# A hybrid decoder layer: experts in a written order per engine, the per-layer-input product moved ahead of the experts, w_out tile by tile

## The chip, the cores and the metric

The kernel runs on one core of a Trainium2 chip. The metric is the device time of one execution in microseconds (us), lower is better. The engines are named as in the profile: PE (TensorE, matrix products and transposes), DVE (VectorE), ACT (ScalarE), POOL (GpSimd, here mostly indirect DMAs) and SP (SyncE, which issues the other DMAs). Each engine works through its own instructions in their order and waits for others by semaphores.

## The reference

One layer over 1024 tokens of width 1024, in float32. After two parallel mixers, which the change leaves alone:

```
x = x + merged @ w_out
h = rmsnorm(x, ln_moe)
group = top-1 of 4 groups; experts = top-2 of its 8 (32 experts in all)
for each chosen expert e:  hid = silu(h @ w_gate[e]) * (h @ w_up[e]);  y = hid @ w_down[e]
x = x + sum over the two experts of weight * y
x = x + sigmoid(rmsnorm(x, ln_ple) @ w_ple_gate) * (p @ w_ple_proj)
out = rmsnorm(x, ln_final)
```

w_out and w_ple_gate are 1024x1024, w_ple_proj is 256x1024, each expert has 1024x512 (gate), 1024x512 (up) and 512x1024 (down).

## The kernel before

A float32 product is made of three passes: each operand is split into a high part (ACT copies it to the rounded type fp32r) and a low part (DVE subtracts the high part from the original), and PE adds high*high, high*low and low*high in PSUM. So each weight passes through ACT (`wh`) and DVE (`wl`) before PE reads it.

**w_out and routing** (`w_out`, L905). 16 products, each of one tile of 128 tokens and one half n of 512 columns (24 matmuls of 512 columns): first all eight tiles with n=0, then all eight with n=1, into PSUM tiles "mm" and "c" in turn, two buffers each. DVE adds the loaded `x` to a product (L931). `route_logits` (L987) transposes the new x on PE and multiplies by the router weights; with n=1 a tile's routing follows (`route_tile`), a long series of small DVE operations that ends in two matmuls `ps_py<-ro,so`. These are generators; one step of each open one runs after every third matmul, and `ROUTE_LAG` puts steps between the parts. After the last tile the indices of the first experts' tokens (`gidx`) exist, and POOL gathers the rows `xg` from DRAM (`h2d`).

**Experts** (`moe`, L1285). Each of 32 experts has at most 88 rows here. The parts run in the order u(e), g(e+1), d(e): up, the next expert's gate, down. Each part is 24 matmuls over four splits of 128x1024 (u0..u3 and so on, six matmuls each); `wh` and `wl` have three buffers each (L1181), so a split may start once the matmuls of the split three earlier are done. Between them PE transposes the next rows (`ps_c<-identk,xg`; ACT copies `xh`, DVE makes `xl`) and the hidden values (`ps_w<-identk,gu`; then `hh`, `hl`). `sg` is the silu of the gate on ACT, `gu` its product with up on DVE. The output `y` is scaled out of PSUM half by ACT (L1242) and half by DVE (L1243), and scattered to DRAM (`yb`). The weights arrive as blocks `mraw` of 2 MB in eight buffers. What stands where on an engine is decided by a scheduler that builds the program, from the order in the code and its own estimates.

**Per-layer-input product.** `ple_in` (L1350) splits p and w_ple_proj and makes 16 products of six matmuls (`ps_c<-wpp,pT`), which ACT scales into `ppo` in SBUF (L1391). It is advanced by `step` inside the expert loop, some of the weight blocks being given up for it (`KEEP`).

**Tail** (L1490 on). w_ple_gate is split to `pgh`, `pgl` (L1485, L1486), the scattered rows are read back (`yin`) and added to x (L1406), and eight tiles are multiplied, gated with `ppo` and normalised.

Of the kernel before, what the change touches and what calls it, by code (L numbers as in the profile page):

```python
# [71 lines left out]
class Kern:  # L72
# [646 lines left out]
    def common(self, ctx):  # L719
# [19 lines left out]
        self.yb = dp.tile([2 * S, D], F32, name="yb")  # L739
        self.ovt = dp.tile([NOV * CAP, 4], F32, name="ovt")  # L740
# [164 lines left out]
    def w_out(self, pool, w, rt):  # L905

        nc, a = self.nc, self.a
        tags = ("mm", "c")
# [9 lines left out]
        for s in range(2 * NT):  # L918
            n, i = s // NT, s % NT
            (wh, wl), tok, sl = w[n], slice(i * 128, i * 128 + 128), slice(n * 512, n * 512 + 512)  # L920
            x = xs[i][n] = pool.tile([128, 512], F32, name="x2", bufs=10)
# [16 lines left out]
            side.append(self.route_logits(pool, rt, i, x, r, n))  # L938
        while side:
            run()  # L940
# [46 lines left out]
    def route_logits(self, pool, rt, i, x, r, q):  # L987

        nc = self.nc
        yield 1  # L990
# [6 lines left out]
        yield 1  # L997
        pl = self.logits[:, 36 * i:36 * i + 36]
        for k in range(4):
            self.mm(pl, hT[:, k, :], self.wr[:, 4 * q + k, :], start=(q == 0 and i == 0 and k == 0),  # L1000
                    stop=(q == 1 and k == 3), skip=True)
        yield 1
        if q == 1:
            yield from self.route_tile(rt, i, r, pl)

    def route_tile(self, rt, i, r, pl):
# [35 lines left out]
        for _ in range(ROUTE_LAG):  # L1042
            yield 1
# [20 lines left out]
        yield 1  # L1064
        yield 1
# [219 lines left out]
    def moe(self, mo, keep):  # L1285
# [5 lines left out]
        raws = [(self.expert_raw(w, z), z) for w, z in zip(order, "1110000x")]  # L1291
        n, free = [8, 0], {"0": 0, "1": 0, "x": 0}

        def raw():

            r, z = raws.pop(0)
            n[1] += 1
            if n[1] > KEEP[z][free[z]]:
                free[z] += 1
            elif n[0] < len(order):  # L1300
                raws.append((self.expert_raw(order[n[0]], z), z))
                n[0] += 1
            return r
        ple = self.ple_in()
        last = [0]

        def step(e):
            if free["1"] > 0 and (last[0] < 1 or e >= last[0] + 3) and (free["1"] > 2 or last[0] == 0):
                if last[0] == 0:
                    last[0] = e  # L1310
                next(ple, None)
# [8 lines left out]
        nx = {}  # L1320

        def rows(e):
            nx["x"] = self.expert_rows(mo, xgs[e % 3])
            gath(e + 3)

        def hidden(e, sg):
            nx["h"] = self.expert_hidden(mo, sg)
        rows(0)
        x = nx["x"]
        sg = self.expert_gate(mo, x, raw())  # L1330
        for e in range(NE):
            more = e + 1 < NE
            sg = self.expert_up(mo, x, raw(), sg, (lambda: rows(e + 1)) if more else None)
            step(e)
            if more:
                x = nx["x"]
                nsg = self.expert_gate(mo, x, raw(), lambda: hidden(e, sg))
            else:
                hidden(e, sg)
            self.expert_down(mo, nx["h"], raw(), self.sidx[:, e:e + 1], self.sw[:, e:e + 1])  # L1340
            sg = nsg
            if e % 3 == 0:
                step(e)
        for _ in ple:
            pass


    def ple_in(self):
# [22 lines left out]
        self.ple = th, tl, hi, lo  # L1371
        self.pps = []
        for i in range(NT):
            if i % 4 == 0:
                ob = self.blk("10"[i // 4], "ppo")
            self.pps.append(ob[:, i % 4 * D:i % 4 * D + D])
            for n in range(2):
                self.ple_proj(i, n)
                yield

    def ple_proj(self, i, n):

        th, tl, wh, wl = self.ple
# [7 lines left out]
        self.nc.scalar.activation(self.pps[i][:, n * 512:n * 512 + 512], p, AF.Copy, scale=0.5)  # L1391
# [76 lines left out]
    def load_pg(self, mo):  # L1468
# [4 lines left out]
        st = self.blk("x", "pgr")  # L1473
        raws = [st[:, n * D:n * D + D] for n in range(4)] + self.xgs + [mo.tile([128, D], F32, name="pgr7", tag="y", bufs=3)]
        prev = self.rawdma
        for k0, k1 in ((0, 6), (6, 8)):
# [3 lines left out]
            for k in range(k0, k1):  # L1480
                if k % 4 == 0:
                    hi, lo = (self.blk("10"[k // 4], f"pg{c}{k}", F32R) for c in "hl")
# [8 lines left out]
    def tail(self, pool, mo, out):  # L1491
        nc, a = self.nc, self.a
        pg = self.load_pg(mo)
        next(pg)
        lnf = mo.tile([128, D], F32, name="lnf", tag="y", bufs=3)
        xs = {0: self.tail_x(pool, mo, 0)}
        pg.send(self.yin)
        nc.sync.dma_start(lnf, a["ln_final"][None, :].to_broadcast([128, D]))
        fr = {0: self.tail_front(pool, mo, *xs.pop(0))}
        xs[1] = self.tail_x(pool, mo, 1)  # L1500
        for i in range(NT):
            if i + 2 < NT:
# [14 lines left out]
    def post_mixer(self, out):  # L1517
        tc, nc = self.tc, self.nc
        with ExitStack() as ctx:
            keep = ctx.enter_context(tc.tile_pool(name="keep", bufs=1))  # L1520
            self.big["1"] = (ctx.enter_context(tc.tile_pool(name="big1", bufs=1)), 3)
            with tc.tile_pool(name="big2", bufs=1) as b2:
# [10 lines left out]
                with tc.tile_pool(name="op", bufs=1, side="right") as op:  # L1533
                    self.w_out(op, w, rt)
# [93 lines left out]
```

## Time and profile before

| | us |
|---|---|
| median of 3 runs | 1698.07 (1697.37 to 1699.02) |
| the profiled execution | 1698.45 |
| its span (first to last instruction) | 1696.6 |
| outside the span | 1.85 |
| PE busy | 1618.1 |
| DVE busy | 1279.7 |
| ACT busy | 863.0 |

Rows of the trace count from the start of the span. The last product of w_out is done at 956, the first matmul of an expert starts at 977, the last expert's down part at 1570, the tail's products at 1591. A matmul's own duration of about 0.39 overlaps its neighbours; what counts is the distance of starts.

### The profile page before, as it was taken

The page shows a single profiled execution, that of the slowest core. Times are in us where ns is not written, and L with a number is a line of the kernel's source. Part 1 is how long each engine was busy: PE and PEld are TensorE (multiplying, and loading weights), DVE is VectorE, ACT ScalarE, POOL GpSimd, SP SyncE. Part 2 cuts the span into 40 slices and gives each one's busy share as a digit, 9 for nine tenths or more (in the row PEclk, how much of TensorE's full clock was granted, in tenths as well). Part 3 has the DMA queues.
Part 4 walks back from the last instruction along what each step waited for, and adds up shares of the span by engine and source line. Part 5 has one row for each costly group of instructions (what it writes and reads, how often), then busy time and mean ns, then how long its engine had stood idle before and what let it go on. Part 6 is the DMA issues. An engine that isn't in the chain of part 4 may idle for free.

```text
span 1696.6 us, 26475 instructions
## 1 busy us (share of the span) xinstructions
PE 1618.1 (95%) x9856; PEld 1225.6 (72%) x9856; DVE 1279.7 (75%) x2636; ACT 863.0 (51%) x1389; POOL 156.5 (9%) x134
## 2 busy tenths in 40 slices
PE   7999999999999999999899699999999999999697
PEld 5877777777787878778687466666666666666586
DVE  7256665377788888666608889999998888899785
ACT  5234333332233333322313388888887777888442
POOL 1000000000000000000002312112211111111000
PEclk9999999999999999999999899999999999999799
DMA  6333222332323323368837689999799989999651
GB/s 191 103 108 100 70 74 82 109 100 79 78 55 94 79 76 88 110 212 267 262 113 265 226 311 335 384 372 380 286 360 349 346 300 349 344 386 362 218 175 50
DMA packets 189030, 349.75 MB, mean 206 GB/s; under 512 B 50862, under 2 KB 123182, under 8 KB 164322
## 3 DMA queue, kind: packets, MB, share of 16 engines
q1 hardware_dynamic: 179682, 331.02, 56.3%
q0 software_dynamic: 9216, 17.01, 3.2%
q8 instruction: 78, 1.28, 0.3%
q14 instruction: 54, 0.44, 0.1%
HBM read 301.10 MB, written 52.95 MB: 209 GB/s over the span
## 4 chain that ended last, share of the span: by engine, by line
PE 81%; DVE 9%; DMA 5%; issue 2%; ACT 2%; SPq 1%; POOL 0%; DVEq 0%; ACTq 0%; POOLq 0%
PE ps_mm L77 47%; PE ps_py L77 16%; PE ps_c L77 9%; PE ps_w L81 4%; PE ps_w L77 4%; PE ps_c L81 1%; DVE so L1068 1%; DMA raw<-in_w_out_dram 1%; DMA ysp<-yaT 1%; DMA mraw<-in_w_up_e_dram 1%; DMA x<-in_x_dram 0%; DMA zr<-zT 0%; DVE wl L1187 0%; ACT sm L337 0%; DMA yb<-y,idx 0%
## 5 line engine op out<-in xcount | busy, mean ns | idle before, releaser
L1187 DVE TENSOR_TENSOR wl<-mraw,wh 128x1024 fp32r<-128x1024 f32 x384 | 457.8, 1220 | 51.0 <-ACT wh L1186 49.9
L1186 ACT ACTIVATE wh<-mraw 128x1024 fp32r<-128x1024 f32 x384 | 402.7, 1058 | 96.0 <-PE ps_mm L77 66.2
L77 PE MATMUL ps_mm<-h,wh 128*128 128x512 f32 x1152 | 378.7, 403 | 0.1
L77 PEld LDWEIGHTS ps_mm<-h,wh 128*128 128x128 f32 x1152 | 214.3, 189 | 47.4 <-issue 1.6
L77 PE MATMUL ps_mm<-h,wl 128*128 128x512 f32 x576 | 231.1, 401 | 0.0
L77 PE MATMUL ps_mm<-wh,xh 128*88 128x512 f32 x512 | 205.3, 401 | 0.0
L77 PE MATMUL ps_mm<-wl,xh 128*88 128x512 f32 x512 | 204.1, 399 | 1.3 <-DVE wl L1187 1.2
L77 PE MATMUL ps_mm<-wh,xl 128*88 128x512 f32 x512 | 201.8, 394 | 0.0
L77 PEld LDWEIGHTS ps_mm<-h,wl 128*128 128x128 f32 x576 | 108.8, 189 | 23.4 <-issue 1.0
L1244 POOL DMA_INDIRECT yb<-y,idx x32 | 71.4, 2230 | 462.6 <-ACT wh L1186 255.0
L77 PEld LDWEIGHTS ps_mm<-wl,xh 128*88 128x88 f32 x512 | 79.4, 155 | 40.5 <-DVE wl L1187 5.0
L77 PEld LDWEIGHTS ps_mm<-wh,xl 128*88 128x88 f32 x512 | 79.4, 155 | 37.2 <-DVE xl L1163 0.2
L77 PEld LDWEIGHTS ps_mm<-wh,xh 128*88 128x88 f32 x512 | 79.3, 155 | 35.0 <-issue 0.4
L77 PE MATMUL ps_py<-wl,hh 128*88 128x512 f32 x256 | 102.7, 401 | 0.0
L77 PE MATMUL ps_py<-wh,hl 128*88 128x512 f32 x256 | 100.3, 393 | 0.5 <-DVE hl L1228 0.5
L77 PE MATMUL ps_py<-wh,hh 128*88 128x512 f32 x256 | 99.4, 393 | 0.6 <-ACT hh L1227 0.6
L102 ACT ACTIVATE wh<-raw 128x1024 fp32r<-128x1024 f32 x44 | 46.6, 1058 | 100.4 <-PE ps_mm L77 95.2
L103 DVE TENSOR_TENSOR wl<-raw,wh 128x1024 fp32r<-128x1024 f32 x42 | 51.3, 1220 | 60.9 <-ACT wh L102 60.5
L77 PEld LDWEIGHTS ps_py<-wl,hh 128*88 128x88 f32 x256 | 39.4, 154 | 27.2 <-DVE wl L1187 10.0
L77 PEld LDWEIGHTS ps_py<-wh,hh 128*88 128x88 f32 x256 | 39.5, 154 | 20.4 <-ACT hh L1227 0.7
L77 PEld LDWEIGHTS ps_py<-wh,hl 128*88 128x88 f32 x256 | 39.5, 155 | 17.9 <-DVE hl L1228 0.9
L77 PE MATMUL ps_mm<-woh,m 128*128 128x512 f32 x128 | 47.0, 417 | 1.3 <-ACT m L93 1.3
(398 smaller groups left out, 2877.5 us busy)
## 6 DMA issues: line engine op xcount, KB each, us to landing
mraw<-in_w_gate_e_dram SPq DMA_DIRECT2D x64, 1024.0 KB, 8.8
mraw<-in_w_up_e_dram SPq DMA_DIRECT2D x64, 1024.0 KB, 8.6
mraw<-in_w_down_e_dram SPq DMA_DIRECT2D x64, 1024.0 KB, 8.5
raw<-in_w_in_dram SPq DMA_DIRECT2D x36, 512.0 KB, 4.1
gT<-t SPq DMA_DIRECT2D x32, 256.0 KB, 2.0
g<-gT SPq DMA_DIRECT2D x32, 256.0 KB, 4.5
yin<-yb SPq DMA_DIRECT2D x16, 512.0 KB, 5.2
zT<-t SPq DMA_DIRECT2D x28, 256.0 KB, 2.0
```

Source lines behind the costliest of these rows:

```text
L77: return self.nc.tensor.matmul(out, l, r, start=start, stop=stop, skip_group_check=skip)
L81: return self.nc.tensor.transpose(out, in_, self.ident[:k, :k])
L102: nc.scalar.activation(wh, raw, AF.Copy)
L103: (eng or nc.vector).tensor_tensor(wl, raw, wh.bitcast(F32), op=ALU.subtract)
L1068: V.tensor_scalar(so, cb[:, CB["iota"]][:, :CAP], pk[:, k:k + 1], None, op0=ALU.is_equal)
L1186: nc.scalar.activation(wh, r, AF.Copy)
L1187: nc.vector.tensor_sub(wl, r, wh.bitcast(F32))
L1244: nc.gpsimd.indirect_dma_start(out=self.yb[:, :], out_offset=bass.IndirectOffsetOnAxis(ap=sidx, axis=0), in_=y, in_offset=None, bounds_che ...
```

## The change

`w_out` now takes both halves of a tile one after the other, all into the PSUM tile "mm", and the lags of the last tile's routing are shorter. Loading and splitting of the per-layer-input operands move into `w_out`; eight of the 16 products are issued beside the end of the routing, the other eight after it, ahead of the experts. Their results go to a DRAM tensor `ppd` by SP and are read back in the tail. In the expert stage every ACT, DVE and PE instruction is chained to the one before it, in the order in which `experts` is written. Both halves of `y` are on ACT and stand three splits after the products that they read. All eight blocks stay with the weights.

```diff
-KEEP = {"1": (29, 36, 36, 999), "0": (50, 999), "x": (0, 999)}
+NP_ROUTE = 8
...
+        self.ple = self.ple_in(pool)
...
-            n, i = s // NT, s % NT
+            n, i = s % 2, s // 2
...
+            if s in (4, 7, 9, 11):
+                next(self.ple)
...
-            p = self.ptile(tags[s % 2])
+            p = self.ptile("mm")
...
+        for _ in range(NP_ROUTE):
+            run()
+            next(self.ple)
...
-        for _ in range(ROUTE_LAG):
+        for _ in range(ROUTE_LAG if i < NT - 1 else 4):
             yield 1
...
-        raws = [(self.expert_raw(w, z), z) for w, z in zip(order, "1110000x")]
+        raws = [(self.expert_raw(order.pop(0), z), z) for z in "0000x111"]
...
+    def seq(self, eng, f, *a, **kw):
+
+        last = self.last.get(eng)
+        with self.tc.issue_after(last) if last else nullcontext():
+            r = f(*a, **kw)
+        self.last[eng] = r.ins
+        return r
...
+        def split(r):
+            wh = mo.tile([128] + list(r.shape[1:]), F32R, name="wh", tag="mwh", bufs=3)
+            wl = mo.tile([128] + list(r.shape[1:]), F32R, name="wl", tag="mwl", bufs=3)
+            act(wh, r, AF.Copy)
+            dve("tensor_sub", wl, r, wh.bitcast(F32))
+            return wh, wl
...
+        for kind, e in todo:
+            more, end = e + 1 < NE, kind == "d" and e + 1 == NE
...
+            for q in range(4):
+                for i in range(q, 3 if end and q == 0 else q + 1):
+                    if i not in ws:
+                        ws[i] = split(r[:, i * st:i * st + st, :])
+                wh, wl = ws[q]
+                if kind == "g" and e:
+                    if q == 0:
+                        rows_out(e)
+                    if q == 2:
+                        gated(e - 1)
+                        hid_tr(e - 1)
+                if kind == "u":
+                    if q == 1 and more:
+                        rows_tr(e + 1)
+                    if q == 2:
+                        y_out(e - 1) if e else silu(0)
+                if kind == "d":
+                    if q == 0:
+                        if end:
+                            gated(e)
+                            hid_tr(e)
+                        hid_out(e)
+                    if q == 2 and more:
+                        silu(e + 1)
...
+        o = pool.tile([128, 512], F32, name="ppo", tag="x2", bufs=8)
+        self.nc.scalar.activation(o, p, AF.Copy, scale=0.5)
+        self.nc.sync.dma_start(self.ppd[i * 128:i * 128 + 128, n * 512:n * 512 + 512], o)
...
+                nc.sync.dma_start(self.pps[i + 1], self.ppd[i * 128 + 128:i * 128 + 256, :])
...
+            for _ in self.ple:
+                pass
             c_rt.close()
```

`rows_out` is xh and xl, `gated` is gu, `hid_tr` the four hidden transposes, `hid_out` hh and hl, `y_out` both halves of y and the scatter.

DVE in one expert in the middle of the stage, before: after `xl` and the split g1 comes `gu`, then g2, g3 and d0 (the `wl` of three splits).

```order
L1163 TENSOR_TENSOR xl<-ps_c,xh 128x352 x2
L1187 TENSOR_TENSOR wl<-mraw,wh 128x1024
L1214 TENSOR_TENSOR gu<-sg,ps_mm 88x512
L1187 TENSOR_TENSOR wl<-mraw,wh 128x1024 x3
L1228 TENSOR_TENSOR hl<-ps_w,hh 128x352
L1187 TENSOR_TENSOR wl<-mraw,wh 128x1024 x5
L1243 TENSOR_SCALAR y<-ps_py,sw 88x512
```

The same place on DVE after: two splits, g1 and g2, stand between `xl` and `gu`, and no `y`.

```order
L1325 TENSOR_TENSOR xl<-ps_c,xh 128x352 x2
L1325 TENSOR_TENSOR wl<-mraw,wh 128x1024 x2
L1325 TENSOR_TENSOR gu<-sg,ps_mm 88x512
L1325 TENSOR_TENSOR wl<-mraw,wh 128x1024 x2
L1325 TENSOR_TENSOR hl<-ps_w,hh 128x352
L1325 TENSOR_TENSOR wl<-mraw,wh 128x1024 x8
```

So `gu`, which the hidden transposes on PE need, stands one split later; PE's own order there (g0, g1, hidden transposes, g2) is the same in both.

PE at the end of the routing, after (`ps_c<-wpp,pT` are the moved products, `ps_py<-ro_9561,so` the last matmuls that the gather's indices need; TENSOR_LOAD reads whether any expert overflowed, and the experts follow):

```order
L78 MATMUL ps_py<-wr,h2T 128x36 x4
L78 MATMUL ps_c<-wpp,pT 128x512 x6
L78 MATMUL ps_py<-ro_9421,so 88x96 x2
L78 MATMUL ps_c<-wpp,pT 128x512 x24
L78 MATMUL ps_py<-ro_9510,cb 128x32
L78 MATMUL ps_py<-C,cb 128x32
L78 MATMUL ps_c<-wpp,pT 128x512 x6
L78 MATMUL ps_py<-ro_9561,so 88x96 x2
L78 MATMUL ps_w<-C,cb 128x32
L78 MATMUL ps_c<-wpp,pT 128x512 x48
L1262 TENSOR_LOAD nover
```

Before, the same rows stand there without the products, so that 48 matmuls are new between the routing's last matmul and the experts. On ACT the first instruction of the experts waits in the new program for the last eight writes of `ppd`.

DVE in the last expert, after (`pgl` are splits of w_ple_gate):

```order
L1325 TENSOR_TENSOR wl<-mraw,wh 128x1024 x2
L1325 TENSOR_TENSOR gu<-sg,ps_mm 88x512
L1585 SCALAR_TENSOR_TENSOR pgl_15495<-pgr,vec,pgh_15494 128x1024
L1585 SCALAR_TENSOR_TENSOR pgl_15505<-xg_9589,vec,pgh_15504 128x1024
L1325 TENSOR_TENSOR hl<-ps_w,hh 128x352
```

Before, `gu` stands there ahead of the two `wl` (the splits d1, d2 of the last expert), and all `pgl` behind `hl`; after, the two `wl` come ahead of `gu` and two `pgl` ahead of `hl`. On ACT three `pgh` likewise stand ahead of the last `hh`.

## Rows read from the trace of the kernel before

**Rows 1.** The page: the chain of work that ended last, share of the span by engine.

```profile
PE 81%; DVE 9%; DMA 5%; issue 2%; ACT 2%; SPq 1%; POOL 0%; DVEq 0%; ACTq 0%; POOLq 0%
```

**Rows 2.** Busy time by stretch (from:to, length, busy time and instructions of PE, PEld, DVE, ACT, POOL, then PE's granted clock, busy share of the DMA engines, GB/s): from the start of expert 0's down part to that of expert 30, and three single experts, the last of which holds two steps of the per-layer-input product.

```profile
997.45:1554.17 556.72, 556.16 (x2625) 376.95 (x2624) 513.34 (x517) 450.74 (x530) 97.09 (x56) 1.00 0.95 351
...
1050.17:1067.95 17.78, 17.78 (x85) 11.92 (x84) 16.84 (x18) 14.61 (x17) 3.40 (x2) 1.00 1.02 384
1067.95:1085.70 17.75, 17.75 (x85) 11.93 (x84) 16.85 (x18) 14.63 (x17) 3.40 (x2) 1.00 1.01 376
1192.23:1212.35 20.12, 19.56 (x95) 13.05 (x93) 19.38 (x20) 17.16 (x21) 7.28 (x2) 1.00 0.60 199
```

**Rows 3.** The timeline of PE in one expert: u0's first matmul, the row transposes, u1's first, g0's first, the hidden transposes, g2's first.

```profile
1073.46 0.39 PE L77 MATMUL ps_mm<-wh,xh 128*88 128x512 f32 x1
...
1076.22 0.77 PE L81 MATMUL ps_c<-identk,xg 88*128 88x88 f32 x8
1076.78 0.45 PE L77 MATMUL ps_mm<-wh,xh 128*88 128x512 f32 x1
...
1079.62 0.39 PE L77 MATMUL ps_mm<-wh,xh 128*88 128x512 f32 x1
...
1082.38 0.47 PE L81 MATMUL ps_w<-identk,gu 88*128 88x88 f32 x4
1082.64 0.44 PE L77 MATMUL ps_mm<-wh,xh 128*88 128x512 f32 x1
```

**Rows 4.** The timelines of ACT and DVE in the same expert.

```profile
1068.48 2.00 ACT L1186 ACTIVATE wh<-mraw 128x1024 fp32r<-128x1024 f32 x2
...
1073.24 0.67 ACT L1242 ACTIVATE y<-ps_py,sw 88x512 f32<-88x512 f32 x1
...
1079.82 1.06 ACT L1186 ACTIVATE wh<-mraw 128x1024 fp32r<-128x1024 f32 x1 [0.33 <-PE ps_mm L77]
...
1074.51 0.74 DVE L1243 TENSOR_SCALAR y<-ps_py,sw 88x512 f32<-88x512 f32 x1
1075.17 3.57 DVE L1187 TENSOR_TENSOR wl<-mraw,wh 128x1024 fp32r<-128x1024 f32 x3
1078.66 0.95 DVE L1163 TENSOR_TENSOR xl<-ps_c,xh 128x352 fp32r<-128x352 f32 x2
...
1080.66 1.07 DVE L1214 TENSOR_TENSOR gu<-sg,ps_mm 88x512 f32<-88x512 f32 x1
```

**Rows 5.** Groups of instructions from 997 to 1554 by line: the products that move, and their copies out of PSUM.

```profile
L77 PE MATMUL ps_c<-wpp,pT 128*128 128x512 f32 x96 | 25.0, 393 | 0.0
...
L1391 ACT ACTIVATE ppo<-ps_c 128x512 f32<-128x512 f32 x16 | 9.6, 597 | 4.3 <-PE ps_c L77 4.3
```

**Rows 6.** The chain of waits in w_out, n=0, and DVE's additions of x: the ninth (the first with n=1) and the 16th.

```profile
834.96 3.86 PE ps_mm L77 x17
838.83 4.77 issue
...
863.65 2.85 PE ps_mm L77 x12
...
870.51 2.84 PE ps_c L77 x12
...
893.96 0.69 DVE L931 TENSOR_TENSOR x<-x,ps_mm 128x512 f32<-128x512 f32 x1 [6.18 <-PE ps_mm L77]
...
956.22 0.69 DVE x L931
```

**Rows 7.** From the routing's end to the first expert: timelines of PE, POOL and ACT, and the median time from issue to landing of the 256 KB writes of h2d and of 1 MB weight loads in 900 to 970.

```profile
968.41 0.94 PE L77 MATMUL ps_py<-ro,so 128*88 128x96 f32 x4 [0.58 <-DVE so L1068]
975.46 1.41 PE L81 MATMUL ps_c<-identk,xg 88*128 88x88 f32 x8 [6.10 <-DMA xg<-h2d,gidx]
976.88 0.70 PE L77 MATMUL ps_mm<-wh,xh 128*88 128x512 f32 x1
...
969.87 1.24 POOL L1146 DMA_INDIRECT xg<-h2d,gidx  x1 [5.21 <-DVE rf L1084]
...
972.53 1.28 ACT L1186 ACT_TABLE_LOAD   x1 [6.88 <-SPq L1252]
...
976.31 0.46 ACT L1162 ACTIVATE xh<-ps_c 128x352 fp32r<-128x352 f32 x1 [1.44 <-PE ps_c L81]
...
h2d<-h SPq DMA_DIRECT2D x16, 256.0 KB, 2.4
...
mraw<-in_w_up_e_dram SPq DMA_DIRECT2D x3, 1024.0 KB, 7.0
```

**Rows 8.** The last expert: DVE, ACT, and from the chain of waits the start of its down part.

```profile
1565.90 1.07 DVE L1214 TENSOR_TENSOR gu<-sg,ps_mm 88x512 f32<-88x512 f32 x1 [0.46 <-PE ps_mm L77]
...
1569.16 0.52 DVE L1228 TENSOR_TENSOR hl<-ps_w,hh 128x352 fp32r<-128x352 f32 x1
1569.60 2.47 DVE L1486 SCALAR_TENSOR_TENSOR pgl<-pgr,vec,pgh 128x1024 fp32r<-128x1024 f32 x2
...
1567.60 0.46 ACT L1227 ACTIVATE hh<-ps_w 128x352 fp32r<-128x352 f32 x1 [0.64 <-PE ps_w L81]
1567.96 2.18 ACT L1485 ACTIVATE pgh<-pgr,vec 128x1024 fp32r<-128x1024 f32 x2
...
1569.74 4.40 PE ps_py L77 x18
```

More of the change, by code (lines that the diff above doesn't have):

```diff
@@ L739, in common @@
         self.yb = dp.tile([2 * S, D], F32, name="yb")
+        self.ppd = dp.tile([S, D], F32, name="ppd")
         self.ovt = dp.tile([NOV * CAP, 4], F32, name="ovt")
@@ L918, in w_out @@
         for s in range(2 * NT):
-            n, i = s // NT, s % NT
+            n, i = s % 2, s // 2
             (wh, wl), tok, sl = w[n], slice(i * 128, i * 128 + 128), slice(n * 512, n * 512 + 512)
-            x = xs[i][n] = pool.tile([128, 512], F32, name="x2", bufs=10)
+            x = xs[i][n] = pool.tile([128, 512], F32, name="x2", bufs=8)
             nc.sync.dma_start(x, a["x"][tok, sl])
+            if s in (4, 7, 9, 11):
+                next(self.ple)
             mh, ml = self.mhi[i // 2], self.mlo[i // 2]
-            p = self.ptile(tags[s % 2])
+            p = self.ptile("mm")
             for k in range(8):
@@ L989, in route_logits @@
         nc = self.nc
-        yield 1
+        last = i == NT - 1 and q == 1
+        for _ in range(1 if last else 4):
+            yield 1
         p = self.ptile()
@@ L996, in route_logits @@
         yield 1
-        yield 1
+        if not last:
+            yield 1
+            yield 1
         pl = self.logits[:, 36 * i:36 * i + 36]
@@ L1063, in route_tile @@
         yield 1
-        yield 1
-        yield 1
+        for _ in range(2 if i < NT - 1 else 0):
+            yield 1
         for k in range(2):
@@ L1290, in moe @@
             order += [wu[e]] + ([wg[e + 1]] if e + 1 < NE else []) + [wd[e]]
-        raws = [(self.expert_raw(w, z), z) for w, z in zip(order, "1110000x")]
-        n, free = [8, 0], {"0": 0, "1": 0, "x": 0}
+        raws = [(self.expert_raw(order.pop(0), z), z) for z in "0000x111"]
         def raw():
             r, z = raws.pop(0)
[L1297 to L1302, printed above, removed]
-            return r
[L1304 to L1311, printed above, removed]
+            if order:
+                raws.append((self.expert_raw(order.pop(0), z), z))
+            return r
         xgs = [t[:CAP] for t in self.xgs]
@@ L1319, in moe @@
             self.overflow(mo, ov)
-        nx = {}
-        def rows(e):
-            nx["x"] = self.expert_rows(mo, xgs[e % 3])
-            gath(e + 3)
[L1326 to L1330, printed above, removed]
-        for e in range(NE):
[L1332 to L1337, printed above, removed]
-            else:
[L1339 to L1343, printed above, removed]
@@ L1350, in ple_in @@
+    def ple_in(self, pool):
         nc, a = self.nc, self.a
@@ L1472, in load_pg @@
         self.pg = []
-        st = self.blk("x", "pgr")
+        st = self.blk("0", "pgr")
         raws = [st[:, n * D:n * D + D] for n in range(4)] + self.xgs + [mo.tile([128, D], F32, name="pgr7", tag="y", bufs=3)]
@@ L1481, in load_pg @@
                 if k % 4 == 0:
-                    hi, lo = (self.blk("10"[k // 4], f"pg{c}{k}", F32R) for c in "hl")
+                    hi, lo = (self.blk(z, f"pg{c}{k}", F32R) for c, z in zip("hl", ("00", "0x")[k // 4]))
                 sl = slice(k % 4 * D, k % 4 * D + D)
@@ L1494, in tail @@
         next(pg)
+        ob = [self.blk("1", f"pp{i}") for i in range(2)]
+        self.pps = [ob[i // 4][:, i % 4 * D:i % 4 * D + D] for i in range(NT)]
         lnf = mo.tile([128, D], F32, name="lnf", tag="y", bufs=3)
@@ L1498, in tail @@
         nc.sync.dma_start(lnf, a["ln_final"][None, :].to_broadcast([128, D]))
+        nc.sync.dma_start(self.pps[0], self.ppd[0:128, :])
         fr = {0: self.tail_front(pool, mo, *xs.pop(0))}
@@ L1501, in tail @@
         for i in range(NT):
+            if i + 1 < NT:
+                nc.sync.dma_start(self.pps[i + 1], self.ppd[i * 128 + 128:i * 128 + 256, :])
             if i + 2 < NT:
@@ L1532, in post_mixer @@
                 nc.vector.tensor_copy(self.ident, self.cb[:, CB["ident"]])
-                with tc.tile_pool(name="op", bufs=1, side="right") as op:
-                    self.w_out(op, w, rt)
+                op = c_rt.enter_context(tc.tile_pool(name="op", bufs=1, side="right"))
+                self.w_out(op, w, rt)
             self.big["x"] = ctx.enter_context(tc.tile_pool(name="bigx", bufs=1)), 1
```

90 lines of the change are left out of this document (77 added, 13 removed).

## The prediction

> **What bounds the kernel now.** I read the page first: the chain that ended last is 81% PE, 9% DVE and 5% DMA [rows 1], so the time goes where PE's products go, and to the places where PE waits. Then the windows by stage. The expert stage, from the down part of expert 0 to that of expert 30, lasts 556.72 us [rows 2]. An expert without the per-layer-input product takes 17.75, in which DVE is busy 16.85 and ACT 14.63: DVE is nearly full too. Thirty such experts make 532.5; the rest, 24.2, is the 16 products and their transposes (96 matmuls [rows 5] at 0.23 are 22.1).
>
> PE's own work in an expert comes from the starts in [rows 3]: 12 matmuls of u0 and u1 in 2.76 (1073.46 to 1076.22), so 0.23 each; 0.56 for the row transposes, 0.26 for the hidden ones. 72 x 0.23 + 0.82 = 17.38, and 0.37 of each expert is waiting. Both prizes of the change are thus known: 24.2 for the products, if they cost nothing elsewhere, and at most 30 x 0.37 = 11 for the order. A change of under 0.2%, 3.4 us, can't be told from none.
>
> **Part 1: the order in the experts.** The products leave: -24.2. What they leave behind depends on the new order, and here the order rows decide: `gu` now stands behind the `wl` of g2. With three buffers, the `wh` of g2 can't start before u3's matmuls are done; it started 0.20 after g0's first matmul (1079.82 against 1079.62) [rows 3, 4]. Before, DVE used that time for `gu` and PE found its hidden transposes ready. After, PE stops at the hidden transposes, with g2, g3 and d behind them on its queue.
>
> How long it stops follows from a chain that begins one part earlier. Count from u0's first matmul. ACT's `wh` of u2 waits for d3's end: 0.20, and takes some 0.95 (a pair took 2.00 and one 1.06). Then come both halves of `y`, 0.57 each by the same overlap (0.67 alone), and only then the `wh` of u3, 1.06: done at 3.35. From 3.40 DVE has no gap: `wl` of u3 and g0 at 1.16 each (three took 1075.17 to 1078.66), `xl` 0.86, `wl` of g1 and g2 at 1.16, `gu` 1.07 [rows 4]. Sum 9.97; with 0.05 to hand over, the transposes start at 10.02. PE is there after 36 x 0.23 + 0.56 = 8.84. So PE waits 1.18 an expert (a part of it already at g1), and the old 0.37 is gone: 17.38 + 1.18 = 18.56. Thirty are 556.8, the stage as long as before: +0.1. The order gives back all that the products' leaving gains.
>
> Bounds. Below: only the `wh` of g2 binds, 0.20 + 1.06 + 0.05 + 1.16 + 1.07 + 0.05 = 3.59 after g0 where PE needs 2.76: 0.83, a period of 18.21, -10.4 for the stage. Above: each of the five hand-overs costs 0.05 more than I took: 18.8, +7.3. The `y` that moves off DVE (0.74) shortens nothing, since DVE's chain begins behind `wh` of u3.
>
> On the transfers: an expert moves 376 GB/s x 17.75 us = 6.67 MB, and one stretch ran at 384 GB/s [rows 2], so 17.4 us is within reach of the DMAs. The Trainium skill, "DMA: Bandwidth & Descriptors", Specifications, gives a core about 358 GB/s of HBM. By that, an estimate from the page's figure, no order could bring an expert under 18.6 us, and rival A below would be impossible. The rows are above the limit, so they decide and I give the rule no weight; my own sum would be the same by it.
>
> **Part 2: w_out and routing.** With n=1 seven products took from 893.96 to 956.22, 8.9 each, where DVE's routing of a tile is the pace; with n=0 the pace is PE's 6.86 (863.65 to 870.51) [rows 6]. Tile by tile, one routing falls on two products, and PE becomes the pace: 7 x 6.86 = 48.0, plus some 0.6 a tile for the routing's small matmuls (an estimate: four of them took 0.94 at the lower clock [rows 7]), 4 in all: 52 in place of 62.3, -10.3. Against it: the third product ran 17 matmuls, 3.86, before the 4.77 us stop at 838.83 [rows 6]. Now it needs the PSUM buffer of the first, which is free only once x is there: +3.9. The last product ends at 949.9 instead of 956.2. The transposes of p fall into that stop and cost nothing.
>
> From there the routing of the last tile took 13.65 to the gather's issue (969.87) [rows 7]. Its latency is DVE's; a product in PE's queue ahead of a routing matmul can hold it by up to its 1.39, and I count one: gather at 964.9, landed by 970.4, 5.0 earlier than before.
>
> **Part 3: eight products before the experts.** They start after the routing's last matmul, which was 1.46 ahead of the gather [rows 7]: at about 964. 48 x 0.23 = 11.1, so PE is free at 975.1; the gather is hidden. Then a new wait: ACT's first expert instruction needs the last `ppd` write. Copy 0.6 [rows 5], write 2.4 (as h2d), 978.1. Then, one behind the other, ACT's table load 1.28, two `xh` 0.84 and a `wh` 1.06; before, the table and the first `wh` were done while the gather ran. First matmul at 981.4, against 976.88: +4.5 [rows 7]. With the first `gu` wait, +5.0 at expert 0's down part. Between products and experts PE is idle some 6 us, as it was for the gather (6.10), so the first matmuls again run at the lower clock and nothing is saved there.
>
> Bounds: +1, if the writes land at once and the routing isn't held; +10, if the writes queue among the weight loads and take 7.0 like these.
>
> **Part 4: the last expert.** Before, `gu` started with the end of u31 (1565.90) and the down part at 1569.74, 3.84 later [rows 8]. After: `wh` and `wl` of d2 first, 0.20 + 1.06 + 0.05 + 1.16, `gu` at 2.47; then two `pgl`, 2.4 together, ahead of `hl` (0.52): 2.47 + 1.0 + 2.43 + 0.52 = 6.4. The three `pgh` ahead of `hh` end at about 4.4 and hide beside it. +2.6; bounds 0 and +4. What follows (scatter, read back, x) hangs on it in full. The tail reads 4.2 MB more, half a megabyte a tile; at the 376 GB/s of [rows 2] that is 1.4 a tile, which I take as hidden beside the tail's products (48 matmuls a tile, 11 us); were it not, it would be 11 in all.
>
> **Sum.** The profiled execution is 1698.45: +5.0 +0.1 +2.6 gives 1706.2; it lies 0.4 above the median, so 1705.8, say 1705.5.
>
> **Rivals.**
> A, faster: PE does not wait for `gu`, since DVE, without `y` and products, runs ahead. Place: the hidden transposes; price: 1.18 x 30 = 35. At PE's own 17.38 the stage takes 521.4, at the old 17.75 532.5: with the other terms 1670 to 1681. For it: DVE's load falls to 16.1 of 17.75. Against it: `wh` of g2 can't start before u3 ends, and DVE is in order. It decides once `gu` is ready within 2.76 of g0's start. Chance 0.15.
> B, no change: only the `wh` of g2 binds, the part from `y` to `wh` of u3 having slack: 18.21, stage -10.4, 1695.3. For it: ACT has 3 us free in an expert, so u3's split may be early. Against it: the `wh` of u2 also waits for a release. Chance 0.2.
> C, slower still: the `ppd` writes land among weight loads, start +10, and the two `pgl` and `pgh` of u31 hold PE by another 1 to 2: 1711 to 1713. For it: weight loads took 7.0 there. Against it: h2d's writes took 2.4 beside the same loads. Chance 0.2.
> The forecast itself has 0.45, and 1700 to 1710 for its own range.
>
> **How the numbers follow.** Faster by over 0.2%: A, a third of B and a little of the forecast, 0.26. Within: the rest of B and the forecast's low end, 0.2. Slower: 0.54. The range 1680 to 1716 leaves out most of A and the far end of C.
>
> **What would show it.** In the trace after: PE idle of about 1 us before each group of hidden transposes, put down to `gu`, and 18.5 between down parts; ACT's first instruction after the routing released by a DMA on `ppd` near 978; the down part of the last expert some 6 after the end of u31; additions of x in w_out 6.9 to 7.2 apart with the last near 950. An expert of 17.4 to 17.75 would make me wrong in part 1, and with it in the sign.

## The result, and the profile after

The changed kernel takes 1718.11 us, the median of 4 runs (1715.84 to 1721.0), beside 1697.72 for the kernel before (4 runs, 1695.65 to 1699.02). The ratio is 1.0122, with a 95% interval of 1.0099 to 1.0145: slower by about 20 us. The forecast was 1705.5, and the range ended at 1716.

The profiled execution of after took 1715.86 (span 1714.0). Its span is 17.4 longer than that of before, and it divides so:

| stretch | before | after | change | forecast |
|---|---|---|---|---|
| to expert 0's down part | 997.45 | 1006.99 | +9.5 | +5.0 |
| from there to expert 30's | 556.72 | 561.61 | +4.9 | +0.1 |
| expert 30's to the last one's | 15.57 | 19.27 | +3.7 | +2.6 |
| the rest of the span | 126.86 | 126.13 | -0.7 | 0 |

(The down parts of experts 0 and 30 are counted from the end of the matmul ahead of them, as in [rows 2]; the last one's is taken from its first matmul with `hl`, 1569.74 in [rows 8] and 1587.87 here.) All three terms have the forecast sign, and all three are larger.

Busy time by stretch (columns as in [rows 2]): the stage, one expert, and two pieces of the first expert's start:

```profile
1006.99:1568.60 561.61, 539.23 (x2521) 355.26 (x2520) 498.24 (x481) 455.86 (x540) 77.05 (x57) 1.00 0.96 355
1063.01:1081.70 18.69, 17.95 (x85) 11.84 (x84) 16.59 (x17) 15.20 (x18) 2.75 (x2) 1.00 1.01 378
984.00:988.00 4.00, 3.48 (x8) 1.99 (x9) 3.40 (x3) 2.10 (x3) 0.00 (x0) 0.50 0.99 348
988.00:992.00 4.00, 4.00 (x14) 2.55 (x13) 1.92 (x2) 1.96 (x3) 0.00 (x0) 0.69 1.02 422
```

In the stage PE, which before was busy for all but 0.6 us, is now idle for 22.4. An expert takes 18.69 here, 561.61 / 30 = 18.72 in the mean, though PE has no product of the per-layer input in it any more.

What PE and its loads waited for in 1000 to 1560 (total, times, longest):

```profile
PEld ps_w L82 <- DVE gu L1325: 35.4, 30, 1.2
PE ps_w L82 <- DVE gu L1325: 21.5, 30, 0.7
PEld ps_mm L78 <- DVE wl L1325: 15.0, 30, 0.6
```

This is the wait that the forecast named: the hidden transposes on `gu`, once in each expert. Its 35.4 / 30 = 1.18 is idle time of PEld, PE's weight loads, at this one place, and no measure of the forecast 1.18, which was PE's whole wait; PE's own is read from its starts. The timeline of PE in one expert, the places of [rows 3]:

```profile
1068.51 0.39 PE L78 MATMUL ps_mm<-wh,xh 128*88 128x512 f32 x1
...
1069.89 0.77 PE L82 MATMUL ps_c<-identk,xg 88*128 88x88 f32 x8
1070.45 0.45 PE L78 MATMUL ps_mm<-wh,xh 128*88 128x512 f32 x1
...
1074.65 0.39 PE L78 MATMUL ps_mm<-wh,xh 128*88 128x512 f32 x1
...
1078.55 0.52 PE L82 MATMUL ps_w<-identk,gu 88*128 88x88 f32 x4 [0.71 <-DVE gu L1325]
1078.86 0.44 PE L78 MATMUL ps_mm<-wh,xh 128*88 128x512 f32 x1
```

From u0's first matmul to the hidden transposes: 1078.55 - 1068.51 = 10.04, where 10.02 was forecast. ACT and DVE in the same expert, the places of [rows 4]:

```profile
1069.68 1.24 ACT L1325 ACTIVATE y<-ps_py,sw 88x512 f32<-88x512 f32 x2
1070.82 1.05 ACT L1325 ACTIVATE wh<-mraw 128x1024 fp32r<-128x1024 f32 x1
1072.07 1.06 ACT L1325 ACTIVATE wh<-mraw 128x1024 fp32r<-128x1024 f32 x1 [0.21 <-PE ps_mm L78]
...
1071.90 2.50 DVE L1325 TENSOR_TENSOR wl<-mraw,wh 128x1024 fp32r<-128x1024 f32 x2 [0.86 <-ACT wh L1325]
1074.31 0.95 DVE L1325 TENSOR_TENSOR xl<-ps_c,xh 128x352 fp32r<-128x352 f32 x2
1075.18 2.35 DVE L1325 TENSOR_TENSOR wl<-mraw,wh 128x1024 fp32r<-128x1024 f32 x2
1077.44 1.05 DVE L1325 TENSOR_TENSOR gu<-sg,ps_mm 88x512 f32<-88x512 f32 x1
```

The series is the forecast one: both `y`, `wh` of u3 (1070.82), then without a gap `wl` of u3 and g0, `xl`, `wl` of g1 and g2, `gu`. Ahead of it DVE idles 0.86. But a second row is as late: the `wh` of g0 (1072.07) waited for PE, for the end of u1's matmuls. It is done at 1073.13, when DVE is done with u3. The experiments below take up this second chain.

The start of the experts, where [rows 7] shows before (timelines of POOL, PE, ACT and SP's queue):

```profile
961.62 1.24 POOL L1157 DMA_INDIRECT xg<-h2d,gidx  x1 [8.98 <-DVE rf L1106]
...
972.69 0.86 PE L82 MATMUL ps_c<-identk,xg 88*128 88x88 f32 x8 [0.41 <-PEq L1263]
983.97 0.70 PE L78 MATMUL ps_mm<-wh,xh 128*88 128x512 f32 x1 [10.42 <-SPq L1263]
...
972.37 0.60 ACT L1489 ACTIVATE ppo<-ps_c 128x512 f32<-128x512 f32 x1 [0.76 <-PEq L1263]
980.81 1.28 ACT L1325 ACT_TABLE_LOAD   x1 [7.84 <-DMA ppd<-ppo]
...
965.25 1.11 SPq L1183 DMA_DIRECT2D mraw<-in_w_up_e_dram  x1
966.45 6.86 SPq L1490 DMA_DIRECT2D ppd<-ppo  x6
```

From the chain of waits there:

```profile
972.99 7.73 DMA ppd<-ppo
```

And the writes issued in 960 to 985 (KB each, median us to landing):

```profile
ppd<-ppo SPq DMA_DIRECT2D x9, 256.0 KB, 9.2
```

The last copy of `ppo` ends at 972.97, its write lands 7.73 later, and only then does ACT begin the experts. SP issued a weight load at 965.25, and the writes of the last six products went out behind it, one every 1.3, beside three gathers: 256 KB took 9.2 in the median, not the 2.4 of `h2d` in [rows 7].

The last expert on DVE, where [rows 8] shows before:

```profile
1580.45 1.28 DVE L1585 SCALAR_TENSOR_TENSOR pgl<-pgr,vec,pgh 128x1024 fp32r<-128x1024 f32 x1
1581.65 2.35 DVE L1325 TENSOR_TENSOR wl<-mraw,wh 128x1024 fp32r<-128x1024 f32 x2
1583.92 1.07 DVE L1325 TENSOR_TENSOR gu<-sg,ps_mm 88x512 f32<-88x512 f32 x1
1584.91 1.27 DVE L1585 SCALAR_TENSOR_TENSOR pgl<-pgr,vec,pgh 128x1024 fp32r<-128x1024 f32 x1
1586.10 1.27 DVE L1585 SCALAR_TENSOR_TENSOR pgl<-xg,vec,pgh 128x1024 fp32r<-128x1024 f32 x1
1587.30 0.52 DVE L1325 TENSOR_TENSOR hl<-ps_w,hh 128x352 fp32r<-128x352 f32 x1
```

`gu` behind two `wl`, `hl` behind two `pgl`, as the order rows said; but a third `pgl` stands ahead of the two `wl` as well, and holds them.

### The profile page after: what moved, and what is told of

Read it like the earlier page. It is cut to its first block, busy times and chain, and to the rows that moved or that the text cites. A ratio compares the mean times of both kernels' runs of the same rounds, so it can differ in the third digit from the quotient of the medians.

```text
span 1714.0 us, 26486 instructions
## 1 busy us (share of the span) xinstructions
PE 1618.4 (94%) x9856; PEld 1217.9 (71%) x9856; DVE 1261.8 (74%) x2604; ACT 884.1 (52%) x1421; POOL 130.3 (8%) x134
## 5 line engine op out<-in xcount | busy, mean ns | idle before, releaser
L1325 DVE TENSOR_TENSOR wl<-mraw,wh 128x1024 fp32r<-128x1024 f32 x384 | 463.6, 1222 | 71.3 <-ACT wh L1325 64.6
L78 PEld LDWEIGHTS ps_mm<-wl,xh 128*88 128x88 f32 x512 | 79.7, 156 | 50.4 <-DVE wl L1325 19.3
L78 PE MATMUL ps_mm<-woh,m 128*128 128x512 f32 x256 | 91.1, 411 | 1.2 <-ACT m L94 1.2
L1157 POOL DMA_INDIRECT xg<-h2d,idx x29 | 31.1, 1071 | 454.5 <-PE ps_c L82 425.2
L1391 POOL DMA_INDIRECT yb<-y,idx x32 | 50.6, 1583 | 94.9 <-ACT y L1325 86.6
L78 PEld LDWEIGHTS ps_mm<-woh,m 128*128 128x128 f32 x256 | 48.5, 190 | 11.2 <-ACT m L94 1.7
## 6 DMA issues: line engine op xcount, KB each, us to landing
mraw<-in_w_down_e_dram SPq DMA_DIRECT2D x64, 1024.0 KB, 10.8
```

Source lines behind the costliest of these rows:

```text
L78: return self.nc.tensor.matmul(out, l, r, start=start, stop=stop, skip_group_check=skip)
L1157: self.nc.gpsimd.indirect_dma_start(out=xg, out_offset=None, in_=self.h2d[:, :], in_offset=bass.IndirectOffsetOnAxis(ap=gidx, axis=0), bou ...
L1325: r = f(*a, **kw)
L1391: nc.gpsimd.indirect_dma_start(out=self.yb[:, :], in_=y, in_offset=None, out_offset=bass.IndirectOffsetOnAxis(ap=self.sidx[:, e:e + 1], ax ...
```

## The experiments

Each kernel is after with the edit shown, unless it says before; times are medians, beside those of the kernel before on the same chip. A period is the mean distance between the down parts of successive experts in the trace.

**gu ahead of g2's split.**

```diff
-                    if q == 2:
+                    if q == 1:
                         gated(e - 1)
+                    if q == 2:
                         hid_tr(e - 1)
```

> The changed kernel with one edit: gu is issued on DVE ahead of the low split of g2 instead of behind it. Theory (PE waits at the hidden transposes because gu stands behind a split that can't start before u3 is done): the wait of some 1.2 us per expert goes, the period falls from 18.73 to 17.4 to 17.8, the stage by 28 to 40 us, the time to some 1678 to 1690. Rival (the stage is held by its weight transfers, 6.7 MB per expert at about 358 GB/s, which makes 18.6 us): the period stays above 18.5 and the wait turns up as ACT waiting for weights. Rival (DVE and ACT are simply full): the wait moves to g2's split, period about 18.3.

1702.1 (10 runs, 1697.16 to 1705.15) beside 1697.52, ratio 1.0023 [1.0013, 1.0033]: 16 us of the loss are back. The period is 18.21, not the 17.4 to 17.8 that I expected; the second rival had the place of the new wait and nearly the number. The waits on `gu` are gone, and another is in their place (waits of 1000 to 1540, twice in each expert):

```profile
PEld ps_mm L78 <- DVE wl L1325: 30.2, 60, 0.6
```

DVE runs the same series in the same time; only its last two members are exchanged:

```profile
1070.62 2.50 DVE L1325 TENSOR_TENSOR wl<-mraw,wh 128x1024 fp32r<-128x1024 f32 x2 [0.86 <-ACT wh L1325]
...
1073.90 1.21 DVE L1325 TENSOR_TENSOR wl<-mraw,wh 128x1024 fp32r<-128x1024 f32 x1
1075.03 1.08 DVE L1325 TENSOR_TENSOR gu<-sg,ps_mm 88x512 f32<-88x512 f32 x1
```

PE needs the `wl` of g2 later than `gu`, by the hidden transposes (0.31) and one matmul (0.23): 0.54, and 18.72 - 18.21 = 0.51. The place of `gu` costs half a microsecond an expert; the rest of the wait belongs to what stands ahead of it.

**Both y behind u3's split.** If the chain through `y` alone set the wait, this should shorten it.

```diff
-                    if q == 2:
-                        y_out(e - 1) if e else silu(0)
+                    if q == 2 and not e:
+                        silu(0)
+                    if q == 3 and e:
+                        y_out(e - 1)
```

> The changed kernel with one edit: both halves of y stand on ACT behind the high split of u3 instead of ahead of it; gu stays behind g2's split. Theory (the chain that makes PE wait begins at u2's high split and runs through y and u3's split): u3's split is 1.1 us earlier, and only the release of g2's split binds, 0.83 + 17.4: period 18.2 to 18.35, the time 11 to 16 us shorter, about 1703 to 1706. Rival (only g2's release binds now): the period stays 18.7 and the time 1716 to 1720.

1718.4 (4 runs) beside 1697.52, ratio 1.0118 [1.0102, 1.0135]; period 18.83, no shorter, near the rival's numbers. The idle 0.86 of DVE has only moved, from u3's `wl` to g0's. ACT and DVE:

```profile
1071.36 1.24 ACT L1325 ACTIVATE y<-ps_py,sw 88x512 f32<-88x512 f32 x2
1072.51 1.05 ACT L1325 ACTIVATE wh<-mraw 128x1024 fp32r<-128x1024 f32 x1
...
1073.58 1.23 DVE L1325 TENSOR_TENSOR wl<-mraw,wh 128x1024 fp32r<-128x1024 f32 x1 [0.86 <-ACT wh L1325]
```

This run alone doesn't separate the causes. The edit left `y` on the way: it now stands ahead of g0's `wh`, which starts behind it without a gap, at 1072.51. But u2's first matmul stands at 1072.18, and in after g0's `wh` started 0.20 behind that one, so that here it could have started no earlier than 1072.38. Without `y` there it would have been only some 0.13 earlier, about what the period grew by (0.11). The chain through `y` gave the right number; whether it was the only one, the next runs show.

**The two chains apart and together.** The second chain is the one seen in after, at the `wh` of g0 (1072.07): in after the row transposes stand after u0 on PE, so u1's matmuls end 0.56 later, and with them comes the buffer that g0's split needs. Before, they stood after u1 [rows 3]. Three edits, in four combinations: G is `gu` early, as above; R puts the row transposes after u1; Y gives half of `y` back to DVE and puts both halves after u1.

```diff
-            for n in range(2):
-                act(y[:, n * 512:n * 512 + 512], pd[n], AF.Copy, scale=self.sw[:, e:e + 1])
+            act(y[:, 0:512], pd[0], AF.Copy, scale=self.sw[:, e:e + 1])
+            dve("tensor_scalar", y[:, 512:1024], pd[1], self.sw[:, e:e + 1], None, op0=ALU.mult)
...
                 if kind == "u":
-                    if q == 1 and more:
+                    if q == 2 and more:
                         rows_tr(e + 1)
-                    if q == 2:
-                        y_out(e - 1) if e else silu(0)
+                    if q == 1 and e:
+                        y_out(e - 1)
+                    if q == 2 and not e:
+                        silu(0)
```

G and R:

> gu ahead of g2's split and the row transposes behind u1; both halves of y stay on ACT ahead of u3's split. Theory (two chains of equal length, so that taking one away leaves the other): period 18.0 to 18.25, as with gu alone (18.21). Rival (the row transposes alone are the second cause): 17.6 to 17.8.

G and Y:

> gu ahead of g2's split and y half on ACT, half on DVE, behind u1; the row transposes stay behind u0. Theory (two chains of equal length): period 18.0 to 18.25, as with gu alone (18.21). Rival (both halves of y on ACT alone are the second cause, as the prediction's chain had it): 17.6 to 17.8.

R and Y, with `gu` late:

> The row transposes behind u1 and y half and half, but gu behind g2's split as in the changed kernel. Theory: both chains are shorter, and only the release of g2's buffer binds, at 0.83 above PE's 17.4: period 18.1 to 18.3. Rival (gu's place is the whole cost of the order): 18.6 to 18.75.

All three:

> The changed kernel with three edits of the written order, which make it that of the kernel before: gu ahead of g2's split, the row transposes behind u1 instead of u0, and y half on ACT, half on DVE, behind u1's split. Theory now (two waits are hidden in the order: gu behind g2's split, 0.5 us; and, with equal length, the chain over both halves of y on ACT and the chain over the row transposes, which put off u1's release of g0's buffer by 0.56): the period falls to 17.6 to 17.8, 30 experts to 528 to 534, the time to 1685 to 1692. Rival (the transfers hold the stage at the 18.2 of the run with gu alone, some 366 GB/s): period 18.2, time 1700 to 1703.

| edits | period | time, ratio |
|---|---|---|
| none (after) | 18.72 | 1718.11, 1.0122 |
| G | 18.21 | 1702.1, 1.0023 |
| G, R | 18.09 | 1700.72 (one run) |
| G, Y | 18.22 | 1699.39 (one run) |
| R, Y | 18.41 | 1710.22 (one run) |
| G, R, Y | 17.64 | 1683.16 beside 1696.03, 0.9916 [0.9899, 0.9934] |

With `gu` early, taking away either chain gains next to nothing (0.12 and nothing), and taking away both gains 0.57. That is how two chains of one length look, and the traces show the one that is left. With G and R, ACT goes from `y` to the `wh` of u3 and g0 without a gap, and DVE waits for the first; with G and Y, the `wh` of g0 waits for u1's matmuls on PE, and DVE for this `wh`:

```profile
1071.19 1.99 ACT L1325 ACTIVATE wh<-mraw 128x1024 fp32r<-128x1024 f32 x2
1072.27 2.36 DVE L1325 TENSOR_TENSOR wl<-mraw,wh 128x1024 fp32r<-128x1024 f32 x2 [0.86 <-ACT wh L1325]
...
1068.53 1.07 ACT L1325 ACTIVATE wh<-mraw 128x1024 fp32r<-128x1024 f32 x1 [0.92 <-PE ps_mm L78]
1069.63 1.23 DVE L1325 TENSOR_TENSOR wl<-mraw,wh 128x1024 fp32r<-128x1024 f32 x1 [0.58 <-ACT wh L1325]
```

Two expectations were narrowly missed: R and Y gave 18.41 where 18.1 to 18.3 was expected, and all three ended 2 us below the expected 1685. In the kernel with all three, PE is idle for 0.36 of 500 us (busy time by stretch):

```profile
1000.00:1500.00 500.00, 499.64 (x2378) 339.77 (x2379) 482.23 (x483) 414.25 (x483) 93.27 (x55) 1.00 1.01 380
```

**The expert loop of before, products still ahead.** `experts` is replaced by the old calls, so that the scheduler sets the order again:

```diff
-        self.experts(mo, raw, xgs, gath)
+        for e in range(NE):
+            more = e + 1 < NE
+            sg = self.expert_up(mo, x, raw(), sg, (lambda: rows(e + 1)) if more else None)
...
+                nsg = self.expert_gate(mo, x, raw(), lambda: hidden(e, sg))
...
+            self.expert_down(mo, nx["h"], raw(), self.sidx[:, e:e + 1], self.sw[:, e:e + 1])
```

> The changed kernel with the expert loop of the kernel before (no written order, y half on DVE); the per-layer products stay ahead of the experts and w_out tile by tile. Theory (the written order costs the difference between 17.75 and 18.73): period 17.75, the stage 29 us shorter, last expert as before (4 us shorter): 1682 to 1689, so the two other parts alone are a gain of 9 to 16 over the kernel before. Rival (the stage's weight transfers or the later start of the experts hold it): period 18.5 or more, time above 1705.

1694.27 (10 runs, 1690.23 to 1698.84) beside 1697.52, ratio 0.9979 [0.9965, 0.9992]. I had expected 1682 to 1689: a miss. The period is near 17.75 with PE full, but only until about 1400:

```profile
1050.00:1100.00 50.00, 50.00 (x240) 33.57 (x239) 47.60 (x50) 41.08 (x49) 10.17 (x6) 1.00 1.02 387
...
1400.00:1450.00 50.00, 47.76 (x228) 31.61 (x227) 44.03 (x45) 38.24 (x46) 7.94 (x7) 1.00 1.00 366
```

From there PE loses 2.3 in 50, some 7 us in three such windows; in the trace `xl` and `gu` there stand in other places between the `wl`. Up to there it shows that the written order and not the products' leaving costs the stage its gain. What in the scheduler makes the late experts different was not followed up.

**The last eight copies in a weight block.** The eighth block is the last to be loaded, so its weights can wait for the writes in place of ACT.

```diff
-        raws = [(self.expert_raw(order.pop(0), z), z) for z in "0000x111"]
+        raws = [(self.expert_raw(order.pop(0), z), z) for z in "0000111x"]
...
+        j = 2 * i + n
+        if j == NP_ROUTE:
+            self.pox = self.blk("x", "ppx")
+        o = (pool.tile([128, 512], F32, name="ppo", tag="x2", bufs=8) if j < NP_ROUTE else
+             self.pox[:, (j - NP_ROUTE) * 512:(j - NP_ROUTE) * 512 + 512])
...
-                    hi, lo = (self.blk(z, f"pg{c}{k}", F32R) for c, z in zip("hl", ("00", "0x")[k // 4]))
+                    hi, lo = (self.blk(z, f"pg{c}{k}", F32R) for c, z in zip("hl", ("00", "01")[k // 4]))
```

> The changed kernel with one edit: the copies of the last eight products lie in a weight block (the one that is filled last) and not in buffers whose place the experts' tiles take. Theory (ACT's first expert instruction waited 7.7 us for the last write of these copies to DRAM): ACT is released by the row transposes near 973, the first expert matmul starts some 7 to 9 us earlier than 984, the time falls by 6 to 9 us. Rival (the experts wait for something else there, the branch or the gather, and the write only came last by little): under 2 us.

1710.85 (4 runs) beside 1697.52, ratio 1.007 [1.0053, 1.0087]: 7.3 less than after. ACT's first instruction and PE's first matmul:

```profile
973.55 1.28 ACT L1325 ACT_TABLE_LOAD   x1 [1.27 <-DMA ppd<-ppx]
...
976.70 0.70 PE L78 MATMUL ps_mm<-wh,xh 128*88 128x512 f32 x1 [3.85 <-ACT wh L1325]
```

Both are 7.3 earlier than in after, with an unchanged period of 18.73. The wait for the writes is thus the whole of this sum, not only a part that something else would replace. The edit also put off a weight load: none is issued between 956.12 and 971.67, and the writes landed faster than the 9.2 of after, in 5.6 in the median (issued in 955 to 976):

```profile
ppd<-ppx SPq DMA_DIRECT2D x7, 256.0 KB, 5.6
```

**w_out alone.** Before, with only the new order of `w_out`, its 8 buffers for x in place of 10, and the new lags of the routing; the cut leaves out those in `route_logits` and at the end of `route_tile`.

```diff
-            n, i = s // NT, s % NT
+            n, i = s % 2, s // 2
...
-            p = self.ptile(tags[s % 2])
+            p = self.ptile("mm")
...
-        for _ in range(ROUTE_LAG):
+        for _ in range(ROUTE_LAG if i < NT - 1 else 4):
             yield 1
```

> The kernel before with the change to w_out and the lags of the routing alone; the per-layer products stay in the expert stage. Theory (PE and not DVE's routing is then the pace of w_out): the last product ends some 6 us earlier, the gather starts 5 to 8 us earlier than 969.9, the time falls by 5 to 8: 1689 to 1692. Rival (the experts wait for their weights, whose loads don't start earlier, or the stall on x costs the gain): within 2 us of before.

1693.29 (5 runs) beside 1698.59, ratio 0.9968 [0.9954, 0.9982]: a gain of 5.3, where 1689 to 1692 was expected. The gather is issued at 959.90, 10.0 earlier than before [rows 7] (9.6 counted from `w_out`'s first matmul), but half of that is lost at once:

```profile
970.72 1.41 PE L81 MATMUL ps_c<-identk,xg 88*128 88x88 f32 x8 [11.43 <-DMA xg<-h2d,gidx]
```

The row transposes start 10.8 after the issue instead of 5.6, and the first matmul is 4.7 earlier (972.14 against 976.88).

**The last expert mended.** `gu` ahead of the splits d1 and d2, and `pgh` and `pgl` held behind `hh` and `hl`.

```diff
+                            for i in (1, 2):
+                                ws[i] = split(r[:, i * st:i * st + st, :])
                         hid_out(e)
...
+                with self.tc.issue_after(self.hid[0]):
+                    nc.scalar.activation(hi[:, sl], raws[k], AF.Copy, scale=g)
...
```

`self.hid` holds the instructions that write `hh` and `hl`; `pgl` is put behind `hl` in the same way.

> The changed kernel with one edit in the last expert: gu ahead of the splits d1 and d2, and all splits of w_ple_gate behind hl. Theory (these held the last down part): from expert 30's down part to expert 31's 15.6 to 17 instead of 19.3, the time 2 to 4 us shorter, 1714 to 1716. Rival (the down part of the last expert waits for its weights or the tail takes the time back): under 1 us.

1715.35 (4 runs, 1709.78 to 1721.15), ratio 1.01 [1.0067, 1.0133]; against after's 1718.11 the times alone can't tell. The trace can: the matmul with `hl` stands at 1583.67 and expert 30's down part at 1568.33, 15.3 in place of 19.3, because DVE goes on at once:

```profile
1579.84 1.07 DVE L1325 TENSOR_TENSOR gu<-sg,ps_mm 88x512 f32<-88x512 f32 x1 [0.36 <-PE ps_mm L78]
1580.83 2.35 DVE L1325 TENSOR_TENSOR wl<-mraw,wh 128x1024 fp32r<-128x1024 f32 x2
1583.10 0.52 DVE L1325 TENSOR_TENSOR hl<-ps_w,hh 128x352 fp32r<-128x352 f32 x1
```

Not all of the 4 us is kept: the rest of the span took 127.83 here and 126.13 in after, so this profile gives 1.7 of them back, part of what the rival said. PE runs the first matmuls of the last down part at the half clock there (0.50 granted in 1586 to 1589), as in after, but not before (1.00 in 1566 to 1574); why was not followed up.

**All of it.** G, R and Y, the weight block for the copies and the mended last expert.

> The changed kernel with all mends together: the three edits of the order, the copies of the last eight products in a weight block, and in the last expert gu ahead of the splits d1 and d2 and the w_ple_gate splits behind hl. Theory (the costs found lie behind one another and add up): 1683 of the order's run, less 7 for the hand-over, less 2 for the last expert: 1671 to 1677, some 20 to 25 below the kernel before. Rival (a new wait takes their place: the weights are then loaded later than they are needed, 17.4 us an expert being near the transfers' pace): 1680 or more.

1674.33 (4 runs, 1672.2 to 1675.07) beside 1698.59, ratio 0.9856 [0.9839, 0.9872]: 24 us faster than before. The period is 17.65; PE has no idle time left in the stage, which moves its data at 381 GB/s:

```profile
997.85:1525.00 527.15, 527.15 (x2512) 358.35 (x2511) 507.83 (x509) 436.81 (x508) 97.84 (x57) 1.00 1.01 381
```

## Why the prediction was right and wrong

**Sign and mechanisms: right.** Each stage lost for the reason given: PE at the hidden transposes on `gu`, ACT's first instruction on the last `ppd` write, `hl` behind `pgl`. The size was wrong: 20.4 by the medians, 7.8 forecast, and 2 outside the range. Two terms of the sum failed above all, the write in part 3 and PE's own work in part 1.

**Part 1, the order.** The wait was nearly right: in the expert shown PE loses 0.26 at g1 and 0.88 at the transposes by its starts, 1.14 where 1.18 was forecast. What failed is the term for PE's own work, "72 x 0.23 + 0.82 = 17.38". The period has two pieces. From u0's first matmul to the hidden transposes the chain sets the time, whatever PE's work there takes: 10.04, forecast 10.02. From the transposes to the next u0 it is PE's work alone: 8.70 in the median of the trace, and by the forecast's terms 36 x 0.23 + 0.26 = 8.54. The four transposes take 0.31 and not 0.26, and the 36 matmuls 0.233 each in the mean (0.28 behind the first, 1078.86). In the kernel with all three edits, where PE has next to no wait, this piece takes 8.71 of 17.64. An error of 0.16 an expert (18.72 against 18.56), but it counts 30 times: it is the 4.8 that the stage missed. The chain behind the number was only half of the truth, as the four combinations showed: the row transposes make a second chain of the same length, and I had not followed the release of g0's buffer. That 10.04 fits 10.02 so well therefore tells nothing against the second chain. Rival B rested on the part from `y` to u3 having slack; with R and Y its condition holds, `gu` still late, and the period is 18.41: B's 18.21, with the same 0.16 added 18.37. Rival A fell, since DVE does not run ahead as long as `gu` stands behind g2's `wl`.

**On the transfers** the rows decided rightly: 381 GB/s were held for 527 us, and a period of 17.64 was reached. The remark that my own sum "would be the same by it" was a slip: the 18.6 named there lies above my 18.56, and the sum by it would have been 1 to 2 us higher.

**Part 2, w_out: right in its sum, by luck.** The runs of the 13 profiles differ in when `w_out` begins (its first matmul lies between 818.1 and 823.4, though PE does the same up to there in all kernels), so it is counted from that matmul, 822.14 before and 819.50 after. The gather comes 142.1 later in place of 147.7, 5.6 earlier, where 5.0 was forecast. But two errors cancel in it. The last addition of x is at 944.58, 125.1 later, where 127.8 was forecast: the last seven products took 51.4, near the 52 forecast (where "4 in all" is 0.6 a product and not, as written, a tile), but the stop on x cost less, since the ninth addition comes only 1.8 later than before and not 3.9. And from there to the gather's issue it took 17.0, where 13.65 + 1.39 = 15.0 was forecast. In the kernel with `w_out` alone it took 13.5, and in all 11 profiles with the products ahead of the experts 17.0, so what the change puts beside the routing holds it by 3.5 and not by 1.4.

**Part 3, the eight products: the step that failed.** "Copy 0.6, write 2.4 (as h2d)": the write took 7.73. From the gather's issue to the landing 13.2 was forecast and 19.1 measured, and 5.3 of the difference is this write. I had put the case in rival C, weighed it with 2.4 for `h2d` "beside the same loads", and chosen by that. The rows of `h2d` don't bear that out: I read a median over 900 to 970 and did not look whether those loads were in flight at the same time. In the trace the `h2d` writes issued with a weight load in flight took 2.3 to 4.6, those without one 2.0 to 2.4, and each pair went out when the one before had landed; in after six writes queue one behind the other, behind a load and gathers. From the first matmul to expert 0's down part it then took 23.0, not 21.1. Before, ACT's table load and the first `wh` lay beside the gather; now `xh` comes first and the splits follow with the matmuls already waiting, at the half clock. How much of the 2.0 is due to this is not shown: with the same code up to there, the run with the last expert mended took 1.3 less for this piece. The two make the 7.2 that the forecast lacked from `w_out` on (187.5 to the down part, where it had 180.3); in the table above 2.6 of it does not show, since after's `w_out` began that much earlier. The median of after lies 2.3 above its profiled run, which would fit, but this was not tested.

**Part 4, the last expert.** 3.7 for 2.6: in the trace three more `pgl` stand in the up part of the last expert, ahead of the `wl` that PE waits for, the part that I had only in rival C. The last of them (1580.45) holds the two `wl` and with them `gu`, which starts 3.3 behind u31's last matmul instead of 2.47. Mended, the stretch takes 15.3, as before (15.57). What follows lost nothing more, and the tail's further reads are hidden, as was taken (-0.7 for the rest of the span).

**What decided the size** is therefore in order: the write (5.3), PE's own work behind the transposes (4.8), the first expert (2.0) and the `pgl` (1.1). Rival C, with its 1711 to 1713, had the first and the last of these; its sum was still short by the period and the first expert.

## What to carry to other kernels

A term that counts thirty times must be taken from a whole period and not from a short stretch: 0.003 in the mean distance of 36 matmuls and 0.05 in a group of transposes were 4.8 us. Where an engine's order is written by hand, follow every buffer that a split waits for: after one chain is shortened, a second of the same length can keep the time as it is, and only the kernel with both edits shows the gain. Moving work off a busy stage is worth what its results don't cost where they leave: a write that the next stage waits for is priced by what else is in flight when it is issued.

## What the runs showed of the hardware

A 256 KB write took several times as long here when the DMA engines were full. In after their busy share was 0.92 to 1.06 by the profile's count from 955 to 980, and the `ppd` writes behind the load of 965.25 landed after 7.7 to 11.1; `h2d`'s writes of the same size took 2.4 in the median [rows 7], in a stretch with a share of 0.57 to 0.92. With the copies in a weight block, where no load of 1 MB stands among them, the writes took 5.6 in the median: the load is a part of it. How the rest divides between the gathers and the writes' own series was not tested.

The gather took 10.8, from its issue to the first row transposes, in the kernel with `w_out` alone, and 5.6 before. In 960 to 965 the DMA engines had a share of 1.01 there (413 GB/s); before, in 970 to 975, it was 0.46 (125 GB/s). That these transfers hold it was not tested by itself.

The first matmuls of the experts ran at the half clock for longer than before. In after, behind 10.42 of idle PE, 984 to 988 has 0.50 granted (1.2 of 2.4 GHz) and 988 to 992 has 0.69, in the rows above. Before, behind 6.10 of idle and the transposes, these two rows:

```profile
976.88:980.00 3.12, 3.12 (x8) 1.98 (x9) 2.70 (x4) 2.39 (x4) 0.00 (x0) 0.52 0.23 42
980.00:984.00 4.00, 4.00 (x20) 2.68 (x19) 3.15 (x4) 3.11 (x4) 1.06 (x1) 1.00 0.28 68
```

The same rows show that the DMAs were then busy for a quarter of the time (42 and 68 GB/s); after, they are full in this stretch (348 and 422 GB/s).
